# More seven-product rows, in alternation, with the weight sums made first

## The chip, the cores and the metric

The kernel runs on one core of a Trainium2 chip. The metric is the device time of one execution in microseconds; where several runs are shown, the median is meant. TensorE appears as PE (matmuls) and PEld (loads of the stationary operand), VectorE as DVE, ScalarE as ACT, GpSimd as POOL, SyncE as SP.

## The reference

One sequence of 256 positions and width 2048 goes through two layers: a retention layer, then a layer with multi-head latent attention, each followed by a squared-ReLU MLP of width 8192. All is float32.

```python
def sq_relu_mlp(h, w1, w2):
    return jnp.square(jax.nn.relu(h @ w1)) @ w2
...
    for layer in range(DEPTH):
        if layer < N_A_LAYERS:
            h = rms_norm(x, norm_mix[layer])
            x = x + retention(h, ret_w_in[layer], ret_w_out[layer], ret_cos, ret_sin)
        else:
            ...
            h = rms_norm(x, norm_mix[layer])
            x = x + mla_attention(h, mla_w_dq[j], mla_q_norm[j], mla_w_uq[j], mla_q_nope_norm[j],
                                  mla_q_pe_norm[j], mla_w_o[j], k_nope, k_pe, v, mla_cos, mla_sin)
        x = x + sq_relu_mlp(rms_norm(x, norm_mlp[layer]), mlp_w1[layer], mlp_w2[layer])
```

Retention has 8 heads (queries and keys of 256, values and gates of 512 a head) and an output product of 4096 x 2048. The weights are streamed from memory once; they make up nearly all of the traffic.

## The kernel before

Every product is made in split precision: each operand is taken apart into a rounded high part and a low part (the rest), and a product is three matmuls, high x high, high x low and low x high. Weights are split as they come in, in `split`: ScalarE rounds (the tile `wh`, line 183) and DVE subtracts (`wl`, line 184).

The big products go through `gemm_pair`: 256 positions by 1024 columns of output at a time, as 2 x 2 blocks (two tiles of 128 positions, two of 512 columns). The contracted dimension is passed in rows of 256, that is two k-tiles of 128 (in each row again 2 x 2 blocks of the weights); 2048 of it are 8 rows, numbered 0 to 7. Each row is one `quad`: one load of 1 MB into a `raw` tile, the splits, and the matmuls. An ordinary row makes 8 block products, 24 matmuls, each streaming 512 columns. A seven-product row uses Winograd's form of Strassen's scheme: 7 block products, 21 matmuls, out of sums of weight blocks (`u`, three DVE instructions, lines 312, 316 and 317) and sums of activation blocks (`with_sums`, lines 392 to 394, then a split; the tiles called `more`), which are made once for each activation tile that needs them. It takes four low splits (three of 1024 columns, one of 512) where an ordinary row takes two. Its partial results go to four further banks (`p1`, `p5`, and `p6` with `p7`), which `pair_out` combines with the others after the last row, in copies on ScalarE and sums on DVE.

Which rows are seven-product rows is given by tuples. `SEVEN` (rows 3, 5, 7) holds for most; the first `u` pair of an MLP, and the second half of the retention output, have 5 and 7 alone, since the sums of earlier rows aren't there in time. The attention products have tuples of their own, which the change leaves.

The stages in order, with the tile names that the profile shows: head 0 of the retention with plain products (`rg`, `rq`, `rk`, `rv`); for heads 1 to 7 query and key products (`rq`, `rk`) and a pair for gate and value (`rp`); after the projection of head 4 the first half of the output product (`ro`, two pairs), at the end the second half; the first MLP; key/value and query projections (`kd`, `dqp`, `dq`, `ku`, `uq`) with the attention; its output product (`wo`, `wop`); the second MLP. An MLP is done in four groups of 2048 hidden columns: two pairs of the up product (`u`, 8 rows each), then two pairs of the down product (`d`, 8 rows each). A down pair adds its result to x in device memory through GpSimd's queue (`to_home`); in the last group the first pair is added to x in SBUF (`into_x`), and the last 1024 columns are made by two plain products with three matmuls per k-tile and position tile (`gemm`, tile `d_acc`, weights `mlp_w2t`), one block of 512 columns after the other. When a block of x is complete, it is squared and summed for the norm, transposed, scaled and split for the next product (`x_block_t`).

Loads of weights are issued on SP's queue, in order. `raw` tiles have 3 buffers, `wh` and `wl` 5 each, `u` tiles 2, activation tiles (`act`) 24, general tiles of 2 KB (`f2k`) 14. Of the 8 banks, `tp` has 2, which transposes share with `p1` and `p5`; `p6`/`p7` share theirs with attention scores. Work that follows a product is put off by a queue that counts rows (`later(n, ...)` is n rows on, `tick` runs what is due, `need` runs it earlier where a product requires it). The framework's scheduler then orders the instructions of each engine, by program order and by what its model takes to be ready; it sets all waits. An engine runs its instructions in that order.

At the start the transposed x is loaded in 8 tiles (`first_inputs`) and split. Tiles 3, 5 and 7 are kept, scaled in place later, and their sums made (`sum_up`).

Of the kernel before, what the change touches and what calls it, by code (L numbers as in the profile page):

```python
# [43 lines left out]
NOPE, ROPE, MV, KVR, QR = 128, 64, 128, 512, 1536  # L44
KV_NBS, Q_NB = (320, 256), 384
GROUPS = (4, 4, 4, 4)
SEVEN = (3, 5, 7)
QUERY, FOUR = (3, 4, 6, 7), (3, 5, 6, 7)
PI = math.pi

# [16 lines left out]
def yoco(ctx: ExitStack, tc: tile.TileContext, a):  # L67
# [112 lines left out]
    def split(h, l, src, scale=None):  # L180

        if scale is None:
            nc.scalar.copy(h, src)  # L183
            nc.vector.tensor_tensor(l, src, h.bitcast(F32), op=ALU.subtract)  # L184
        else:
            nc.scalar.activation(h, src, AF.Copy, scale=scale)
            nc.vector.scalar_tensor_tensor(
                l, src, scale, h.bitcast(F32), op0=ALU.mult, op1=ALU.subtract
            )

    def split_act(v, src, scales=(None, None)):
        if scales == (None, None):
# [60 lines left out]
    def gemm_t(w, chunk0, act, nk, name, done):  # L253
# [3 lines left out]
        for g in range(n):  # L257
# [19 lines left out]

            stream(w, chunk0 + g, 2048, f"{name}{g}", use, (lambda: done(acc)) if g == n - 1 else None)

    def quad(w, chunk, x, mm, name):  # L280

        raw = pool.tile([P, 2048], F32, tag="raw", bufs=3, name=f"{name}_raw")
        nc.sync.dma_start(raw, w[chunk])
        v, more = x

        def a(t, k):
            return [v[:, k, i, t * P : (t + 1) * P] for i in range(2)]

        def s(n):
            return [more[:, n // 2, i, n % 2 * P : (n % 2 + 1) * P] for i in range(2)]  # L290

        def parts(src, n, part):
            wh = pool.tile([P, 1024], F32R, tag="wh", bufs=5, name=f"{name}_wh{part}")
            wl = pool.tile([P, 1024], F32R, tag="wl", bufs=5, name=f"{name}_wl{part}")
            split(wh[:, : n * 512], wl[:, : n * 512], src)
            return [[i[:, j * 512 : (j + 1) * 512] for i in (wh, wl)] for j in range(n)]

        if more is None:
            b11, b22 = parts(raw[:, 0:1024], 2, 0)
            mm("c11", a(0, 0), b11)  # L300
            mm("c21", a(1, 0), b11)
            mm("c12", a(0, 1), b22)
            mm("c22", a(1, 1), b22)
            b12, b21 = parts(raw[:, 1024:], 2, 1)
            mm("c12", a(0, 0), b12)
            mm("c22", a(1, 0), b12)
            mm("c11", a(0, 1), b21)
            mm("c21", a(1, 1), b21)
            return
        b11, b22 = parts(raw[:, 0:1024], 2, 0)  # L310
        u = [pool.tile([P, 2, 512], F32, tag="us", bufs=2, name=f"{name}_u{i}") for i in range(2)]
        nc.vector.tensor_tensor(
            u[0], raw[:, 0:1024].rearrange("p (i n) -> p i n", i=2),
            raw[:, 1024:1536].unsqueeze(1).to_broadcast([P, 2, 512]), op=ALU.add,
        )
        nc.vector.tensor_tensor(u[1][:, 0], u[0][:, 0], raw[:, 512:1024], op=ALU.add)
        nc.vector.tensor_tensor(u[1][:, 1], u[1][:, 0], raw[:, 1536:], op=ALU.add)  # L317
        mm("p1", a(0, 0), b11)
        mm("c12", s(3), b22)
        (b21,) = parts(raw[:, 1536:], 1, 1)  # L320
        mm("c11", a(0, 1), b21)
        u2, u4 = parts(u[1].rearrange("p i n -> p (i n)"), 2, 2)
        mm("c21", a(1, 1), u4)
        mm("p6", s(2), u2)
        u1, u3 = parts(u[0].rearrange("p i n -> p (i n)"), 2, 3)
        mm("p5", s(1), u1)
        mm("p7", s(0), u3)
# [243 lines left out]
    def first_inputs(c):  # L571

        t = f2k([2, S], f"x0t_{c}")
        nc.sync.dma_start(t, a["xt"][:, 2 * c : 2 * c + 2, :])
        v = act_tile(f"a0_{c}")
        split_act(v, t, [gain(G_MIX0 + 2 * c + j) for j in range(2)])
        act0.append(v)
        sums0.append(None)
        if c in SEVEN:

            def sum_up():
                for j in range(2):
                    nc.scalar.activation(t[:, j], t[:, j], AF.Copy, scale=gain(G_MIX0 + 2 * c + j))
                sums0[c] = with_sums(t, f"a0s_{c}")

            later(9 + c, sum_up)

# [68 lines left out]
    def ret_out(h, s, v, gate, y_act):  # L656
        o = two_banks(f"o{h}")
        ys = []
        for t in range(NT):
            for m in range(t + 1):  # L660
                lo = m * S + (t - m) * P
                sh, sl = (i[:, lo : lo + P] for i in s)
                vh, vl = v[m]
                nc.tensor.matmul(o[:, t], sh, vh, start=m == 0, stop=False)
                nc.tensor.matmul(o[:, t], sh, vl, start=False, stop=False)
                nc.tensor.matmul(o[:, t], sl, vh, start=False, stop=m == t)
        for t in range(NT):
            so = small(1, f"so{h}{t}")
            square_sum(o[:, t], so, f"o{h}{t}")
            ro = rstd(so, RDV, 1, f"o{h}{t}")  # L670
            y = f2k([512], f"y{h}{t}")
            nc.vector.scalar_tensor_tensor(y, o[:, t], ro, gate[t], op0=ALU.mult, op1=ALU.mult)
            ys.append(y)

        def turn():
            for k2 in range(2):
                tp = transposed(lambda t, j: ys[t][:, (2 * k2 + j) * P : (2 * k2 + j + 1) * P], f"ytp{h}{k2}")
                yt = act_tile(f"y{h}{k2}")
                more = None
                if len(y_act) in (SEVEN if h < RH // 2 else SEVEN[1:]):  # L680
# [12 lines left out]
    into_n1 = into_next(ss, [G_MLP0], [act], r, "n1", SEVEN)  # L693
    halves = [[], []]

    def ret_projected(h, qk, gate, v, s):
# [18 lines left out]
    def ret_out_half(i):  # L715

        w = a["ret_w_out"]
        if i:
            x_tiles("ro")
        for p in range(2):  # L720
            first = SEVEN[1:] if i else SEVEN

            def done(c, p=p):
                into_x(into_n1, c, p) if i else to_home(c, p)

            gemm_pair(w, p * 16 + 8 * i, halves[i], [k in first for k in range(8)], f"ro{i}{p}", done)

    for h in range(RH):
# [32 lines left out]
        if h == RH // 2:  # L761
            ret_out_half(0)
        need(r0, NT)
        while None in [sums0[k] for k in SEVEN]:
            run_first()
        gemm_pair(a["ret_w_gv"], (h - 1) * 8, list(zip(act0, sums0)), [k in SEVEN for k in range(8)], f"rp{h}", paired)
    ret_out_half(1)


    def mlp(layer, act, r, done):  # L770
        w1, w2 = a[f"mlp_w1_{layer}"], a[f"mlp_w2_{layer}"]
        f0 = 0
        for gi, nf in enumerate(GROUPS):
            hid, blocks = [], []
            kinds = [i in SEVEN for i in range(2 * nf)]
            last = gi == len(GROUPS) - 1

            def up(c, p, hid=hid, blocks=blocks):

                need(r, NT)  # L780
                c = summed(c)
                for t in range(NT):
                    for i in range(2):
                        nc.scalar.activation(c[t][i], c[t][i], AF.Relu, scale=r[t])

                def turn(i):
                    for q in (2 * i, 2 * i + 1):
# [8 lines left out]
                        blocks.append((v, with_sums(u, name) if len(blocks) in SEVEN else None))  # L796
                        hid.append(v)

                later(0, lambda: turn(0))
                later(1, lambda: turn(1))  # L800

            for p in range(f0 // 2, (f0 + nf) // 2):
                seven = SEVEN if p else SEVEN[1:]
                gemm_pair(
                    w1, p * 8, act, [i in seven for i in range(8)], f"u{layer}_{p}", lambda c, p=p, up=up: up(c, p)
                )
            if last:
                x_tiles(f"mlp{layer}")
            for p in range(2):
                if last and p:  # L810
                    for b in (2, 3):
                        need(hid, 2 * nf)
                        gemm(
# [5 lines left out]
                def add(c, p=p, last=last):  # L819
                    into_x(done, c, p) if last else to_home(c, p)  # L820

                gemm_pair(w2, p * 32 + 2 * f0, blocks, kinds, f"d{layer}_{gi}{p}", add)
            f0 += nf

# [245 lines left out]
    for b in range(8):  # L1070
# [3 lines left out]
    act, r = [], []  # L1074
    x_tiles("wo")
    gemm_blocks(
        a["mla_w_o"], lambda b: b * 4, a["mla_w_op"], o_act, KD, "wo", into_next(ss, [G_MLP1], [act], r, "n3", SEVEN)
    )

    def finish(b, acc):  # L1080
# [101 lines left out]
```

## Time and profile before

| | |
|---|---|
| runs | 2503.47, 2499.87, 2497.53 us; median 2499.87 |
| profiled execution | span 2497.0 us (the page gives no other time for it) |
| PE, PEld, DVE, ACT, POOL busy | 2471.9, 2075.1, 2096.7, 1574.8, 252.2 us |
| granted TensorE clock | 0.998 of full speed on average |
| memory | 478.09 MB read, 39.85 MB written |

The span is the time from the first to the last instruction of one execution. Busy times are the union of an engine's instructions. The recorded duration of a matmul (390 ns with 512 columns) is longer than the distance between two of them, since they are pipelined; the same holds, by less, for DVE's and ScalarE's instructions in a row. In a timeline "x3" stands for three instructions one after the other, and brackets show the idle time of the engine before an instruction and what ended it.

### The profile page before, as it was taken

The numbers are of one execution on the slowest core, as the hardware profiler recorded it, in microseconds if no ns is written. First come the engines' busy times: TensorE is split into PE (matmuls) and PEld (weight loads), VectorE is DVE, ScalarE is ACT, GpSimd is POOL, SyncE is SP. The second block draws the span as 40 slices with busy tenths as digits, with TensorE's granted clock in tenths as the row PEclk, the third lists the DMA queues.
The fourth block names the chain that finished last, engine by engine and source line by source line (L and its number), as shares of the span: only waits on it lengthen the run. The fifth ranks groups of instructions, "written<-read, shape, count | busy, mean of one in ns | idle before, by whom it ended". The sixth has DMA issues, their size and how long they took to land.

```text
span 2497.0 us, 31492 instructions
## 1 busy us (share of the span) xinstructions
PE 2471.9 (99%) x11683; PEld 2075.1 (83%) x11683; DVE 2096.7 (84%) x2723; ACT 1574.8 (63%) x2228; POOL 252.2 (10%) x308
## 2 busy tenths in 40 slices
PE   8999999999999999999999999999999999999999
PEld 7788888888888888888888888998888888888887
DVE  7788888888898888889889888776899888898896
ACT  6566555555676657566666767666676566575663
POOL 6300011000010110110110101110010201101100
PEclk9999999999999999999999999999999999999999
DMA  8545568555565685775875555444455956857754
GB/s 290 211 173 202 178 217 246 183 193 196 211 217 189 207 263 186 235 237 186 247 259 191 197 196 189 159 149 163 173 213 203 262 203 213 249 187 233 258 200 165
DMA packets 92825, 519.97 MB, mean 208 GB/s; under 512 B 11009, under 2 KB 12161, under 8 KB 39425
## 3 DMA queue, kind: packets, MB, share of 16 engines
q1 hardware_dynamic: 71280, 471.78, 52.5%
q0 software_dynamic: 21248, 46.15, 8.9%
q8 instruction: 91, 1.49, 0.2%
q14 instruction: 62, 0.50, 0.1%
q10 hardware_dynamic: 144, 0.05, 0.0%
HBM read 478.09 MB, written 39.85 MB: 207 GB/s over the span
## 4 chain that ended last, share of the span: by engine, by line
PE 80%; DVE 10%; DMA 4%; ACT 4%; issue 2%; POOL 1%; ACTq 0%; SPq 0%; DVEq 0%; POOLq 0%
PE u_c L353 7%; PE u_c L354 7%; PE u_c L352 7%; PE d_c L353 4%; PE d_c L354 4%; PE d_c L352 4%; PE rp_c L353 3%; PE rp_c L354 3%; PE rp_c L352 3%; DVE d_wl L184 3%; PE ro_c L352 2%; PE ro_c L353 2%; PE ro_c L354 2%; PE rq_acc L272 2%; PE rk_acc L272 2%; DMA d_raw<-in_mlp_w 2%
## 5 line engine op out<-in xcount | busy, mean ns | idle before, releaser
L184 DVE TENSOR_TENSOR u_wl<-u_raw,u_wh 128x1024 fp32r<-128x1024 f32 (+1 forms) x256 | 280.0, 1124 | 35.8 <-ACT u_wh L183 35.8
L184 DVE TENSOR_TENSOR d_wl<-d_raw,d_wh 128x1024 fp32r<-128x1024 f32 (+1 forms) x256 | 283.4, 1132 | 26.0 <-ACT d_wh L183 25.1
L353 PE MATMUL u_c<-u_wl,n 128*128 128x512 f32 x748 | 291.8, 390 | 1.1 <-DVE u_wl L184 1.0
L352 PE MATMUL u_c<-u_wh,n 128*128 128x512 f32 x748 | 291.3, 391 | 0.0
L354 PE MATMUL u_c<-u_wh,n 128*128 128x512 f32 x748 | 291.3, 389 | 0.0
L183 ACT CAST u_wh<-u_raw 128x1024 fp32r<-128x1024 f32 (+1 forms) x256 | 238.9, 981 | 60.6 <-DMA u_raw<-in_mlp_w 27.2
L183 ACT CAST d_wh<-d_raw 128x1024 fp32r<-128x1024 f32 (+1 forms) x256 | 240.0, 991 | 56.3 <-DMA d_raw<-in_mlp_w 25.1
L353 PE MATMUL d_c<-d_wl,hid 128*128 128x512 f32 x644 | 251.4, 390 | 1.7 <-DVE d_wl L184 1.6
L352 PE MATMUL d_c<-d_wh,hid 128*128 128x512 f32 x644 | 252.1, 391 | 0.0
L354 PE MATMUL d_c<-d_wh,hid 128*128 128x512 f32 x644 | 250.9, 390 | 0.0
L183 ACT CAST u_wh<-u_u 128x1024 fp32r<-128x1024 f32 x92 | 94.2, 1050 | 153.5 <-DVE u_u L317 129.8
L183 ACT CAST d_wh<-d_u 128x1024 fp32r<-128x1024 f32 x84 | 84.9, 1049 | 162.6 <-DVE d_u L317 154.7
L353 PEld LDWEIGHTS u_c<-u_wl,n 128*128 128x128 f32 x748 | 140.5, 188 | 31.1 <-DVE u_wl L184 2.8
L354 PEld LDWEIGHTS u_c<-u_wh,n 128*128 128x128 f32 x748 | 140.4, 188 | 29.2
L352 PEld LDWEIGHTS u_c<-u_wh,n 128*128 128x128 f32 x748 | 140.4, 188 | 28.6
L183 ACT CAST rp_wh<-rp_raw 128x1024 fp32r<-128x1024 f32 x112 | 106.7, 972 | 67.7 <-PE rp_c L354 37.5
L184 DVE TENSOR_TENSOR u_wl<-u_u,u_wh 128x1024 fp32r<-128x1024 f32 x92 | 110.7, 1222 | 43.6 <-ACT u_wh L183 43.5
L353 PEld LDWEIGHTS d_c<-d_wl,hid 128*128 128x128 f32 x644 | 120.9, 188 | 29.0 <-DVE d_wl L184 4.5
L354 PEld LDWEIGHTS d_c<-d_wh,hid 128*128 128x128 f32 x644 | 120.9, 188 | 25.1
L352 PEld LDWEIGHTS d_c<-d_wh,hid 128*128 128x128 f32 x644 | 120.9, 188 | 24.6
L184 DVE TENSOR_TENSOR d_wl<-d_u,d_wh 128x1024 fp32r<-128x1024 f32 x84 | 99.9, 1222 | 35.9 <-ACT d_wh L183 35.9
L148 POOL DMA_DIRECT2D xh<-d_c x48 | 42.1, 1029 | 844.6 <-ACT d_c L369 844.5
(567 smaller groups left out, 6570.0 us busy)
## 6 DMA issues: line engine op xcount, KB each, us to landing
u_raw<-in_mlp_w SPq DMA_DIRECT2D x128, 1024.0 KB, 5.3
d_raw<-in_mlp_w SPq DMA_DIRECT2D x112, 1024.0 KB, 4.9
rp_raw<-in_ret_w_gv SPq DMA_DIRECT2D x56, 1024.0 KB, 4.9
ro_raw<-in_ret_w_out SPq DMA_DIRECT2D x32, 1024.0 KB, 4.9
uq_raw<-in_mla_w_uq SPq DMA_DIRECT2D x24, 768.0 KB, 4.1
rq_raw<-in_ret_w_qk SPq DMA_DIRECT2D x16, 1024.0 KB, 6.6
rk_raw<-in_ret_w_qk SPq DMA_DIRECT2D x16, 1024.0 KB, 4.8
d_raw<-in_mlp_w2t SPq DMA_DIRECT2D x16, 1024.0 KB, 5.1
```

The lines of the kernel that those rows point to most:

```text
L148: nc.gpsimd.dma_start(x_home[t][2 * p + j], part, accum_op=ALU.add)
L183: nc.scalar.copy(h, src)
L184: nc.vector.tensor_tensor(l, src, h.bitcast(F32), op=ALU.subtract)
L272: nc.tensor.matmul(acc[f], wh[:, cols], a.rearrange("p i s -> p (i s)"), start=k == 0, stop=k == nk - 1)
L352: nc.tensor.matmul(dst, ah, bh, start=n == 0, stop=False)
L353: nc.tensor.matmul(dst, ah, bl, start=False, stop=False)
L354: nc.tensor.matmul(dst, al, bh, start=False, stop=n == total[key] - 1)
```

## The change

1. Further tuples: `LATE` (5, 7), `ODD` (1, 3, 5, 7), `HEAD` (2, 4, 6, 7). `LATE` is what `SEVEN[1:]` was.
2. Retention: the gate and value pairs and the first half of the output product take `HEAD` instead of `SEVEN`. The sums of x at the start are made for tiles 2, 4, 6 and 7, and the tile is loaded a second time for it rather than kept.
3. MLP, up: pairs 1, 3, 5 and 7 keep `SEVEN`, pairs 2, 4 and 6 take `ODD`, pair 0 has `LATE` as before. MLP, down: the first pair of a group keeps `SEVEN`, the second takes `ODD`. Activation sums are made for `ODD`, that is one more in each group and one more for the input of each MLP.
4. The end of the first MLP: its last 1024 columns are made by a pair with `LATE` instead of two plain products, and go to x as those of the first pair do. The second MLP ends as before.
5. In a seven-product row the three sums of weights are written first, and the first two low splits get an edge that orders them behind the last sum on DVE. It is an order alone and no semaphore.

```diff
-SEVEN = (3, 5, 7)
+SEVEN, LATE, ODD, HEAD = (3, 5, 7), (5, 7), (1, 3, 5, 7), (2, 4, 6, 7)
...
+    def queued_behind(ins, before):
+        tc.add_manual_dep(
+            ins.ins, before.ins.name,
+            mybir.DependencyInfo(mybir.DependencyClass.NoSync, mybir.DependencyReason.DATA), reason="order",
+        )
...
-        def parts(src, n, part):
+        def parts(src, n, part, after=None):
             wh = pool.tile([P, 1024], F32R, tag="wh", bufs=5, name=f"{name}_wh{part}")
             wl = pool.tile([P, 1024], F32R, tag="wl", bufs=5, name=f"{name}_wl{part}")
-            split(wh[:, : n * 512], wl[:, : n * 512], src)
+            low = split(wh[:, : n * 512], wl[:, : n * 512], src)
+            if after is not None:
+                queued_behind(low, after)
...
-        b11, b22 = parts(raw[:, 0:1024], 2, 0)
         u = [pool.tile([P, 2, 512], F32, tag="us", bufs=2, name=f"{name}_u{i}") for i in range(2)]
...
-        nc.vector.tensor_tensor(u[1][:, 1], u[1][:, 0], raw[:, 1536:], op=ALU.add)
+        summed_up = nc.vector.tensor_tensor(u[1][:, 1], u[1][:, 0], raw[:, 1536:], op=ALU.add)
+        b11, b22 = parts(raw[:, 0:1024], 2, 0, summed_up)
         mm("p1", a(0, 0), b11)
         mm("c12", s(3), b22)
-        (b21,) = parts(raw[:, 1536:], 1, 1)
+        (b21,) = parts(raw[:, 1536:], 1, 1, summed_up)
...
-        if c in SEVEN:
+        if c in HEAD:
 
             def sum_up():
+                again = f2k([2, S], f"x0s_{c}")
+                nc.sync.dma_start(again, a["xt"][:, 2 * c : 2 * c + 2, :])
...
-                seven = SEVEN if p else SEVEN[1:]
+                seven = SEVEN if p % 2 else ODD if p else LATE
...
-                if last and p:
+                if last and p and layer:
...
+                kinds = [i in ((LATE if last else ODD) if p else SEVEN) for i in range(2 * nf)]
                 gemm_pair(w2, p * 32 + 2 * f0, blocks, kinds, f"d{layer}_{gi}{p}", add)
```

More of the change, by code (lines that the diff above doesn't have):

```diff
@@ L183, in split @@
             nc.scalar.copy(h, src)
[L184 to L189, printed above, removed]
+            return nc.vector.tensor_tensor(l, src, h.bitcast(F32), op=ALU.subtract)
+        nc.scalar.activation(h, src, AF.Copy, scale=scale)
+        return nc.vector.scalar_tensor_tensor(
+            l, src, scale, h.bitcast(F32), op0=ALU.mult, op1=ALU.subtract
+        )
     def split_act(v, src, scales=(None, None)):
@@ L278, in gemm_t @@
             stream(w, chunk0 + g, 2048, f"{name}{g}", use, (lambda: done(acc)) if g == n - 1 else None)
+    def queued_behind(ins, before):
+        tc.add_manual_dep(
+            ins.ins, before.ins.name,
+            mybir.DependencyInfo(mybir.DependencyClass.NoSync, mybir.DependencyReason.DATA), reason="order",
+        )
     def quad(w, chunk, x, mm, name):
@@ L578, in first_inputs @@
         sums0.append(None)
-        if c in SEVEN:
+        if c in HEAD:
             def sum_up():
+                again = f2k([2, S], f"x0s_{c}")
+                nc.sync.dma_start(again, a["xt"][:, 2 * c : 2 * c + 2, :])
                 for j in range(2):
-                    nc.scalar.activation(t[:, j], t[:, j], AF.Copy, scale=gain(G_MIX0 + 2 * c + j))
-                sums0[c] = with_sums(t, f"a0s_{c}")
+                    nc.scalar.activation(again[:, j], again[:, j], AF.Copy, scale=gain(G_MIX0 + 2 * c + j))
+                sums0[c] = with_sums(again, f"a0s_{c}")
             later(9 + c, sum_up)
@@ L679, in turn @@
                 more = None
-                if len(y_act) in (SEVEN if h < RH // 2 else SEVEN[1:]):
+                if len(y_act) in (HEAD if h < RH // 2 else LATE):
                     u = f2k([2, S], f"yu{h}{k2}")
@@ L692, in yoco @@
     act, r = [], []
-    into_n1 = into_next(ss, [G_MLP0], [act], r, "n1", SEVEN)
+    into_n1 = into_next(ss, [G_MLP0], [act], r, "n1", ODD)
     halves = [[], []]
@@ L720, in ret_out_half @@
         for p in range(2):
-            first = SEVEN[1:] if i else SEVEN
+            first = LATE if i else HEAD
             def done(c, p=p):
@@ L763, in yoco @@
         need(r0, NT)
-        while None in [sums0[k] for k in SEVEN]:
+        while None in [sums0[k] for k in HEAD]:
             run_first()
-        gemm_pair(a["ret_w_gv"], (h - 1) * 8, list(zip(act0, sums0)), [k in SEVEN for k in range(8)], f"rp{h}", paired)
+        gemm_pair(a["ret_w_gv"], (h - 1) * 8, list(zip(act0, sums0)), [k in HEAD for k in range(8)], f"rp{h}", paired)
     ret_out_half(1)
@@ L774, in mlp @@
             hid, blocks = [], []
-            kinds = [i in SEVEN for i in range(2 * nf)]
             last = gi == len(GROUPS) - 1
@@ L795, in turn @@
                         split_act(v, u)
-                        blocks.append((v, with_sums(u, name) if len(blocks) in SEVEN else None))
+                        blocks.append((v, with_sums(u, name) if len(blocks) in ODD else None))
                         hid.append(v)
@@ L1076, in yoco @@
     gemm_blocks(
-        a["mla_w_o"], lambda b: b * 4, a["mla_w_op"], o_act, KD, "wo", into_next(ss, [G_MLP1], [act], r, "n3", SEVEN)
+        a["mla_w_o"], lambda b: b * 4, a["mla_w_op"], o_act, KD, "wo", into_next(ss, [G_MLP1], [act], r, "n3", ODD)
     )
@@ L1168 @@
         arrays[f"mlp_w2_{i}"] = _quads(g["mlp_w2"][i])
-        arrays[f"mlp_w2t_{i}"] = _chunks(g["mlp_w2"][i][-512 * GROUPS[-1] :, 1024:], 512)
+    arrays["mlp_w2t_1"] = _chunks(g["mlp_w2"][1][-512 * GROUPS[-1] :, 1024:], 512)
     arrays = {n: np.ascontiguousarray(v) for n, v in arrays.items()}
```

## Prediction

> **What bounds the kernel now.** I read the page first, then busy time by stage, then one stretch of eleven microseconds instruction by instruction, and last the waits. From the page:
>
> ```profile
> span 2497.0 us, 31492 instructions
> PE 2471.9 (99%) x11683; PEld 2075.1 (83%) x11683; DVE 2096.7 (84%) x2723; ACT 1574.8 (63%) x2228; POOL 252.2 (10%) x308
> ...
> PE 80%; DVE 10%; DMA 4%; ACT 4%; issue 2%; POOL 1%; ACTq 0%; SPq 0%; DVEq 0%; POOLq 0%
> ```
>
> PE is busy throughout, and the chain that ended last is PE for 80% and DVE for 10%. So fewer matmuls are worth their time, as long as DVE, the second engine, still delivers. Busy time by stage, for one head's gate and value pair, the first half of the retention output, two `u` pairs, two `d` pairs (columns: window, length, then busy time and instructions of each engine):
>
> ```profile
> core 0: us, PE busy (x) PEld busy (x) DVE busy (x) ACT busy (x) POOL busy (x), PEclk, DMA share, GB/s
> 464.00:507.00 43.00, 43.00 (x196) 35.72 (x195) 34.09 (x41) 23.53 (x30) 0.00 (x0) 1.00 0.49 181
> 312.00:397.00 85.00, 85.00 (x383) 70.59 (x382) 69.65 (x80) 49.13 (x61) 9.52 (x12) 1.00 0.70 221
> 906.00:991.00 85.00, 85.00 (x385) 70.56 (x384) 73.81 (x82) 54.02 (x70) 4.73 (x6) 1.00 0.66 219
> 991.00:1076.00 85.00, 84.97 (x382) 69.92 (x381) 74.90 (x87) 54.34 (x71) 9.14 (x11) 1.00 0.72 227
> ```
>
> PE fills every stage at full clock; DVE has 10 to 11 us of 85 left in the MLP. Whether those are free is seen in the timeline of DVE, over one ordinary and one seven-product row of a `d` pair:
>
> ```profile
> 1012.64 3.49 DVE L184 TENSOR_TENSOR d_wl<-d_raw,d_wh 128x1024 fp32r<-128x1024 f32 x3
> 1016.04 1.22 DVE L312 TENSOR_TENSOR d_u<-d_raw 128x1024 f32<-128x1024 f32 x1
> 1017.18 0.68 DVE L184 TENSOR_TENSOR d_wl<-d_raw,d_wh 128x512 fp32r<-128x512 f32 x1
> 1017.78 0.68 DVE L316 TENSOR_TENSOR d_u<-d_u,d_raw 128x512 f32<-128x512 f32 x1
> 1018.50 0.69 DVE L317 TENSOR_TENSOR d_u<-d_u,d_raw 128x512 f32<-128x512 f32 x1
> 1020.38 2.36 DVE L184 TENSOR_TENSOR d_wl<-d_u,d_wh 128x1024 fp32r<-128x1024 f32 x2 [1.19 <-ACT d_wh L183]
> 1022.66 3.49 DVE L184 TENSOR_TENSOR d_wl<-d_raw,d_wh 128x1024 fp32r<-128x1024 f32 x3
> ```
>
> The three low splits at the start are two of the ordinary row and the first of the seven-product row: 3.40 us to the next start, 1.13 each. The last sum (L317) ends at 1019.19; then DVE idles 1.19 us, because ScalarE can only now round the sums, and ScalarE had itself waited for them:
>
> ```profile
> 1019.30 2.00 ACT L183 CAST d_wh<-d_u 128x1024 fp32r<-128x1024 f32 x2 [4.74 <-DVE d_u L317]
> ```
>
> Period of DVE for the two rows: 1022.66 - 1012.64 = 10.02 us, 8.83 of it work. The same two rows on PE:
>
> ```profile
> 1014.25 0.39 PE L352 MATMUL d_c<-d_wh,hid 128*128 128x512 f32 x1
> ...
> 1019.69 0.39 PE L352 MATMUL d_p<-d_wh,hid 128*128 128x512 f32 x1
> 1019.91 0.39 PE L353 MATMUL d_p<-d_wl,hid 128*128 128x512 f32 x1
> ...
> 1021.95 0.39 PE L353 MATMUL d_c<-d_wl,hid 128*128 128x512 f32 x1
> ...
> 1024.45 0.39 PE L352 MATMUL d_c<-d_wh,hid 128*128 128x512 f32 x1
> ```
>
> The ordinary row starts at 1014.25, the seven-product row at 1019.69, the next row at 1024.45: 5.44 us for 24 matmuls, 4.76 us for 21, 0.2267 us a matmul, 10.20 together. So in alternating rows DVE's 10.02 us barely keep up with 10.20: the low part of the sums is finished at about 1021.6 (the first of the two splits that begin at 1020.38), and PE uses it at 1021.95. The 10% of DVE in the chain are such stretches. More seven-product rows alone would not fit; the order of the sums has to make room.
>
> **The matmuls removed.** Seven-product rows, before and after: gate and value pairs 7 x 3 to 7 x 4 (+7); first half of the retention output 2 x 3 to 2 x 4 (+2); `u`, per layer, 2 + 7 x 3 = 23 to 2 + 4 x 3 + 3 x 4 = 26 (+3, both layers +6); `d` of the first layer 7 x 3 = 21 to 4 x 3 + 3 x 4 + 2 = 26 (+5); `d` of the second 21 to 24 (+3). That is 23 rows, three matmuls fewer in each: 69 x 0.2267 = 15.6 us off PE. Two of the 23 are in the pair at the end of the first MLP, whose other 6 rows have as many matmuls as the two plain products they replace (2 x 96 against 186).
>
> **What DVE gets for it.** From the timeline a seven-product row costs DVE 1.13 + 1.14 + 0.60 + 0.72 + 0.69 + 2.28 = 6.56 us, an ordinary one 2.27: 4.29 more for each added row. A further set of activation sums costs, by the rows of its four steps,
>
> ```profile
> L392 DVE TENSOR_TENSOR hid_sum<-hid_u 128x256 f32<-128x256 f32 x24 | 10.0, 418 | 0.0
> L393 DVE TENSOR_TENSOR hid_sum<-hid_sum,hid_u 128x128 f32<-128x128 f32 x24 | 6.8, 284 | 0.0
> L394 DVE TENSOR_TENSOR hid_sum<-hid_u,hid_sum 128x128 f32<-128x128 f32 x24 | 6.8, 284 | 0.0
> L184 DVE TENSOR_TENSOR hid_more<-hid_sum,hid_more 128x512 fp32r<-128x512 f32 x24 | 16.4, 685 | 0.0
> ```
>
> 0.42 + 0.28 + 0.28 + 0.69 = 1.67 us; there are 12 more of them (one in each of the eight MLP groups, one each for x0, y and the inputs of the two MLPs). Take a group of the MLP, two `u` and two `d` pairs: PE 170.0 - 2 x 0.68 = 168.6 us; DVE 73.8 + 74.9 + 2 x 4.29 + 1.67 = 159.0. It fits with 9.6 us to spare, which is 0.69 us for each of the 14 seven-product rows in it. A gate and value stage: DVE 34.1 + 4.3 = 38.4 of 42.3. ScalarE has 54 of 85 busy and gets some 1.5 us more a row (two casts of 1.00 more, 0.5 less): no bound.
>
> **The order of the sums.** The new edges put the sums ahead of the row's first two low splits. ScalarE then rounds the raw blocks while DVE adds, and rounds the sums while DVE makes the two low splits (1.13 + 0.60 = 1.73 us against 1.00 for the first cast). The idle 1.19 us has work in it, and two alternating rows cost DVE 8.83 us instead of 10.02, against 10.20 on PE. This is the cover for everything above. In the page's terms, these waits go:
>
> ```profile
> DVE u_wl L184 <- ACT u_wh L183: 79.4, 82, 2.4
> DVE d_wl L184 <- ACT d_wh L183: 60.9, 68, 2.5
> ```
>
> What is queued behind the sums on DVE: the row's low splits, then the next row's, then the sums of `pair_out`. Waiting for that are PE's second matmul in the row, and SP's next load, as its slot of `raw` is free only when two low splits and three sums have read it; that is 1.13 + 1.14 + 0.60 + 0.72 + 0.69 = 4.3 us into the row, before and after. PE's second matmul gets its operand later by the three sums (1.14 + 0.60 + 0.69 = 2.43 us): it was ready at 1016.13 (third split of the group), it is used at 1019.91. 3.8 us of lead become 1.4. Nothing is lost here, but this is where a smaller lead would show.
>
> DVE is tightest where a pair with 1,3,5,7 follows another: rows 7, 0, 1 with the four sums of `pair_out` between (128x512 like L316, some 0.6 each) cost 2 x 6.56 + 2.27 + 2.4 = 17.8 us against 4.76 + 5.44 + 4.76 = 15.0. The 2.8 us come out of the lead, which the alternating rows before it raise by 10.20 - 8.83 = 1.4 us per two rows. Stalls on PE there: between -3 us (those of today go) and +5 over the kernel; I take -1, as the cadence is the nearest row.
>
> **The end of the first MLP.** Now blocks 2 and 3 end together. The nearest rows are the end of the retention output, a pair, and of today's plain product (PE's last matmul, then the last add to x, then the first scaled tile of block 3 for the key/value product):
>
> ```profile
> 733.28 0.39 PE L354 MATMUL ro_p<-ro_wh,y_more 128*128 128x512 f32 x1
> ...
> 742.97 0.68 DVE L461 TENSOR_TENSOR x_ro<-ro_p,x_ro 128x512 f32<-128x512 f32 x1
> ...
> 1423.43 0.39 PE L246 MATMUL d_acc<-d_wh,hid 128*128 128x512 f32 x1
> 1423.65 0.30 PE L244 MATMUL kd_acc<-kd_wh,n 128*128 128x320 f32 x1
> ...
> 1424.32 0.68 DVE L461 TENSOR_TENSOR x_mlp<-d_acc,x_mlp 128x512 f32<-128x512 f32 x1
> ...
> 1427.17 1.04 PE L203 MATMUL n_tp<-cst,x_mlp 128*128 128x128 f32 x8
> ...
> 1429.89 0.48 DVE L187 SCALAR_TENSOR_TENSOR n<-n_tp,gains,n 128x256 fp32r<-128x256 f32 x1 [0.54 <-ACT n L186]
> ```
>
> A pair's x is complete 10.0 us after its last matmul (743.65 - 733.67), a plain product's 1.2 (1425.00 - 1423.82), and a scaled tile follows 5.4 us later (1430.37). So block 3 is late by 8.8 us. As cover, PE has the key/value product of blocks 0 and 1: 24 matmuls took 3.52 us (1423.65 to 1427.17), so 48 take 7.0, and as much again less a fifth in the second, narrower one. Nothing if both are drawn ahead; up to 8 us if PE keeps the order written. I take 3, nearer to the end at which the scheduler moves work, as it did with the low splits above.
>
> **The start.** Four tiles of x are loaded again (256 KB each) on SP, ahead of weights, where three were kept. SP's wait for the sums there goes:
>
> ```profile
> SPq L283 <- DVE a0s_sum L393: 10.1, 1, 10.1
> ```
>
> but the new loads can wait for a free f2k slot. From -1 to +3; I take 0.
>
> Sum: 2497.0 - 15.6 - 1 + 3 = 2483.4 for the span. The median of the runs, 2499.9, is 2.9 above the span; the page has no other time for the profiled run. Forecast 2486.3; by the low ends (-3, 0, -1) 2480, by the high ones (+5, +8, +3) 2500.
>
> **The rivals.** (1) The waits stay. If the reordered row still costs DVE more than 0.69 us of waiting (today 1.19), DVE becomes the bound of the MLP, and each tenth above that costs 8 groups x 14 rows x 0.1 = 11 us. At 1.0 us that is 35 over the forecast: 2521. For it: the edge gives only an order, and a scheduler that lays other work between keeps the ping-pong. Against it: all that the casts need is ready 1.7 us earlier. At 0.8 us, 12 us are lost and no gain can be measured: 2499.
>
> (2) The first low part is late. DVE runs its queue in order, so a row entered with under 2.4 us of lead pays the rest. 84 seven-product rows lie in pairs or stages that get a fourth one (48 in the MLPs, 28 and 8 in the retention); at 0.3 us each that is 25 us, 2511. It decides from 0.19 us a row on. Against it: leads like the 3.8 us above.
>
> (3) DVE's instructions cost their recorded 1.22 us and not the 1.13 between starts, that is 159.0 x 1.08 = 171.7 us in a group of 168.6 on PE: 8 x 3.1 = 25 us lost, 2511. The Trainium skill, "VectorE: DVE Perf Modes", section on the DRAIN that can't be avoided, has the next instruction start only when the pipe is empty (unless it is not held, a case that its next section adds); its fp32 two-tensor formula, (N+151)/0.96, gives 1224 ns for 1024 elements. The recorded 1.22 agrees with the formula, the spacing of 1.13 does not agree with the rule, and the spacing is measured.
>
> (4) The tail and the start take their high ends (8 and 3): 2494.
>
> **How the numbers follow.** About 0.2%, 5 us, is what a measurement of this kernel can tell from no change. Forecast with its bounds 0.70 (all of it faster); rival 1 0.13 (half of it within 0.2%, half slower); rival 2 0.08 (0.06 slower, 0.02 within); rival 3 0.03 slower; rival 4 0.06 (0.03 faster, 0.03 within). Faster 0.73, same 0.11, slower 0.16 by rounding. The range goes from 2479, just under the low ends, to 2505; what lies outside is most of the slower cases and 0.03 below.
>
> **What would show it.** PE 69 instructions of 128x512 fewer in the pairs; in the timeline of DVE the three sums ahead of the row's low splits and no wait for ScalarE before the splits of the sums; the waits of `u_wl` and `d_wl` for `u_wh` and `d_wh` much below 140 us together; DVE near 2200 us busy; a `u` pair stage some 0.7 us shorter for each added row. Wrong: gaps on PE before the second matmul of a seven-product row (rival 2), DVE idle behind ScalarE still (rival 1), a gap of over 5 us in the key/value product.

## Result and profile after

| | before | after |
|---|---|---|
| median of the runs, us | 2499.93 (2497.34 to 2503.47) | 2501.86 (2492.71 to 2505.62) |
| ratio | | 1.0006, 95% interval 0.9996 to 1.0017 |
| profiled execution, us | span 2497.0 | 2504.95, span 2503.2 |
| granted clock | 0.998 | 0.997 |

No change that can be measured; the forecast was 2486.3. From the page of the changed kernel, its totals and the shares of the chain that ended last:

```profile
span 2503.2 us, 31661 instructions
PE 2458.7 (98%) x11614; PEld 2065.5 (83%) x11614; DVE 2199.6 (88%) x2892; ACT 1647.8 (66%) x2297; POOL 252.0 (10%) x308
PE 76%; DVE 12%; DMA 7%; issue 2%; ACT 2%; POOL 1%; DVEq 0%; SPq 0%; ACTq 0%; POOLq 0%
```

PE has the 69 instructions less (11683 to 11614), yet the span of this execution is 6.2 us longer (it is one of the slower of twelve; the medians differ by 1.9). In the chain PE's share fell from 80% to 76%, and DMA's rose from 4% to 7%. Cut at PE's first matmul into `u_c`, its first into `kd_acc`, its next into `u_c` and the end of its last, the two executions compare so (us; "forecast" is the number of added seven-product rows by 0.68, and the +3 of the pair at the end; the -1 for stalls had no place):

| part | before | after | change | forecast |
|---|---|---|---|---|
| retention | 733.5 | 728.2 | -5.3 | -6.1 |
| first MLP | 690.1 | 694.8 | +4.7 | -5.4 |
| key/value, query, attention | 381.0 | 381.9 | +0.9 | +3 |
| second MLP | 688.2 | 693.7 | +5.5 | -4.1 |

So the loss lies in the MLPs, 19.7 us against the forecast for the two. By stages (16 rows, two `u` or two `d` pairs, from PE's first matmul of one to that of the next), a `u` stage that now holds a pair with 1,3,5,7 took 84.76 us before where PE had no gap (in the first MLP 84.76, 84.76 and 86.27). With one row more and no gap it would take 84.08. In the first MLP the three of them took 86.20, 88.39 and 89.17. Busy time in stretches of the first two and of the `d` stage behind them; the columns are those of the prediction's table:

```profile
901.00:987.00 86.00, 84.18 (x380) 69.55 (x379) 77.30 (x89) 57.48 (x73) 4.68 (x6) 1.00 0.67 216
1073.00:1161.00 88.00, 85.78 (x379) 70.46 (x379) 78.36 (x91) 57.27 (x72) 4.43 (x6) 0.98 0.65 212
1161.00:1245.00 84.00, 84.00 (x380) 69.69 (x379) 78.48 (x93) 57.68 (x73) 9.07 (x11) 1.00 0.75 228
```

In the `d` stage PE is busy without a gap; it took 84.09 us. In the two `u` stages PE is idle for 1.8 and 2.2 us, and DVE, which is what PE waits for, has 9 to 10 us idle in each. What ended the idle time (columns: who waited, at which line, and for what; us in total, times, longest):

```profile
DVE d_wl L184 <- ACT d_wh L183: 30.7, 31, 3.0
DVE u_u L318 <- DMA u_raw<-in_mlp_w: 30.0, 17, 4.4
DVE u_wl L184 <- ACT u_wh L183: 26.5, 29, 1.5
DVE d_u L318 <- DMA d_raw<-in_mlp_w: 25.6, 16, 3.5
PE u_c L360 <- DVE u_wl L184: 11.7, 6, 3.1
PE d_c L360 <- DVE d_wl L184: 7.8, 5, 2.4
```

and the four rows of before that answer to the last ones:

```profile
DVE u_u L312 <- DMA u_raw<-in_mlp_w: 6.9, 9, 3.0
DVE d_u L312 <- DMA d_raw<-in_mlp_w: 2.3, 4, 0.8
PE d_c L353 <- DVE d_wl L184: 1.6, 4, 0.5
PE u_c L353 <- DVE u_wl L184: 1.0, 2, 0.8
```

The waits for ScalarE's casts went as predicted, 140.3 us to 57.2. In their place the first sum of a seven-product row (L318) waits for its load: 9.2 us became 55.6. And PE waits for low parts: 2.6 us became 19.5. One such place in the timeline of DVE, then ScalarE, PE, and the pieces of the chain there:

```profile
1087.94 2.35 DVE L184 TENSOR_TENSOR u_wl<-u_u,u_wh 128x1024 fp32r<-128x1024 f32 x2
1093.12 1.23 DVE L318 TENSOR_TENSOR u_u<-u_raw 128x1024 f32<-128x1024 f32 x1 [2.82 <-DMA u_raw<-in_mlp_w]
1094.38 0.69 DVE L322 TENSOR_TENSOR u_u<-u_u,u_raw 128x512 f32<-128x512 f32 x1
1094.99 2.35 DVE L184 TENSOR_TENSOR u_wl<-u_raw,u_wh 128x1024 fp32r<-128x1024 f32 x2
1097.26 0.68 DVE L323 TENSOR_TENSOR u_u<-u_u,u_raw 128x512 f32<-128x512 f32 x1
1097.86 1.82 DVE L184 TENSOR_TENSOR u_wl<-u_raw,u_wh 128x1024 fp32r<-128x1024 f32 x2
```

```profile
1089.13 1.06 ACT L183 CAST u_wh<-u_raw 128x1024 fp32r<-128x1024 f32 x1 [0.73 <-PE u_c L361]
1090.45 1.05 ACT L183 CAST u_wh<-u_raw 128x1024 fp32r<-128x1024 f32 x1 [0.26 <-PE u_c L361]
```

```profile
1093.65 0.39 PE L359 MATMUL u_c<-u_wh,n 128*128 128x512 f32 x1
1096.26 0.51 PE L360 MATMUL u_c<-u_wl,n 128*128 128x512 f32 x1 [2.23 <-DVE u_wl L184]
```

```profile
1084.99 8.04 DMA u_raw<-in_mlp_w
...
1093.12 1.24 DVE u_u L318
```

PE waits 2.23 us for the first of the two splits at 1094.99. They belong to the ordinary row before the seven-product row. ScalarE had cast that row by 1090.19 and 1091.50, so its low splits could have run from 1090.3 on, when DVE became idle. But the scheduler had put the first two sums of the next row ahead of them, and DVE takes its queue in order: it waited until 1093.1 for a load of 1 MB that took 8.04 us, with ready work behind the wait. The last sum (L323) came behind those splits after all, so the row's sums are not even together. All eleven pauses of PE for low parts in the MLPs have this pattern: a load of 7.3 to 9.6 us, then the first two sums (L318, L322), then the ready splits, and PE goes on 3.2 us after the load has landed. In before, the splits of the ordinary row stand ahead of the sums (the prediction's timeline, 1012.64).

### The profile page after: what moved, and what is told of

Its sections match the earlier page's. It is cut to its first block, busy times and chain, and to the rows that moved or that the text cites. A ratio compares the mean times of both kernels' runs of the same rounds, so it can differ in the third digit from the quotient of the medians.

```text
span 2503.2 us, 31661 instructions
## 1 busy us (share of the span) xinstructions
PE 2458.7 (98%) x11614; PEld 2065.5 (83%) x11614; DVE 2199.6 (88%) x2892; ACT 1647.8 (66%) x2297; POOL 252.0 (10%) x308
## 4 chain that ended last, share of the span: by engine, by line
PE 76%; DVE 12%; DMA 7%; issue 2%; ACT 2%; POOL 1%; DVEq 0%; SPq 0%; ACTq 0%; POOLq 0%
PE u_c L360 6%; PE u_c L361 6%; PE u_c L359 6%; PE d_c L360 4%; PE d_c L361 4%; PE d_c L359 4%; DMA d_raw<-in_mlp_w 3%; DVE d_wl L184 3%; DMA u_raw<-in_mlp_w 3%; PE rp_c L360 2%; PE rp_c L359 2%; PE rp_c L361 2%; PE rq_acc L271 2%; PE rk_acc L271 2%; DVE u_wl L184 2%
## 5 line engine op out<-in xcount | busy, mean ns | idle before, releaser
L360 PE MATMUL u_c<-u_wl,n 128*128 128x512 f32 x712 | 280.0, 393 | 11.7 <-DVE u_wl L184 11.7
L359 PE MATMUL u_c<-u_wh,n 128*128 128x512 f32 x712 | 280.4, 395 | 0.0
L361 PE MATMUL u_c<-u_wh,n 128*128 128x512 f32 x712 | 279.1, 392 | 0.0
L360 PE MATMUL d_c<-d_wl,hid 128*128 128x512 f32 x660 | 258.1, 391 | 7.8 <-DVE d_wl L184 7.8
L359 PE MATMUL d_c<-d_wh,hid 128*128 128x512 f32 x660 | 259.1, 393 | 0.0
L361 PE MATMUL d_c<-d_wh,hid 128*128 128x512 f32 x660 | 257.6, 390 | 0.0
L183 ACT CAST u_wh<-u_u 128x1024 fp32r<-128x1024 f32 x104 | 107.8, 1054 | 115.2 <-PE u_c L361 59.2
L183 ACT CAST d_wh<-d_u 128x1024 fp32r<-128x1024 f32 x100 | 103.6, 1055 | 101.0 <-DVE d_u L323 57.5
L361 PEld LDWEIGHTS u_c<-u_wh,n 128*128 128x128 f32 x712 | 134.9, 189 | 28.2
L359 PEld LDWEIGHTS u_c<-u_wh,n 128*128 128x128 f32 x712 | 134.8, 189 | 27.4
L361 PEld LDWEIGHTS d_c<-d_wh,hid 128*128 128x128 f32 x660 | 124.3, 188 | 25.8
L359 PEld LDWEIGHTS d_c<-d_wh,hid 128*128 128x128 f32 x660 | 124.3, 188 | 25.3
L184 DVE TENSOR_TENSOR u_wl<-u_u,u_wh 128x1024 fp32r<-128x1024 f32 x104 | 124.2, 1220 | 9.8 <-ACT u_wh L183 9.8
L184 DVE TENSOR_TENSOR rp_wl<-rp_raw,rp_wh 128x1024 fp32r<-128x1024 f32 x112 | 118.9, 1090 | 3.8 <-ACT rp_wh L183 3.2
```

What stands on the lines that cost most here:

```text
L184: return nc.vector.tensor_tensor(l, src, h.bitcast(F32), op=ALU.subtract)
L359: nc.tensor.matmul(dst, ah, bh, start=n == 0, stop=False)
L360: nc.tensor.matmul(dst, ah, bl, start=False, stop=False)
L361: nc.tensor.matmul(dst, al, bh, start=False, stop=n == total[key] - 1)
```

## Theories

**A**: the loss is this place of the sums, ahead of ready splits of the row before, together with loads that land late. **B**: DVE has too much work with the added rows. **C**: three load buffers are too few, since slots come free later. The expectations below use these letters.

## Experiments

Intervals are 95%, and each ratio is to the kernel before on the same chip.

**1. The sums behind the row before.** One more edge of the same kind: the first sum of a row is ordered behind the last low split of the row before.

```diff
+    row_before, low_split = [None], [None]
...
+        row_before[0] = low_split[0]
...
+            low_split[0] = low
...
-        nc.vector.tensor_tensor(
+        first_sum = nc.vector.tensor_tensor(
...
+        if row_before[0] is not None:
+            queued_behind(first_sum, row_before[0])
```

> The changed kernel with one more order edge: the first sum of a seven-product row stands behind the last low split of the row before it. Theory A (the sums were moved ahead of low splits of the row before, whose operands are ready, and DVE then waits for the load of the seven-product row with these splits behind it): DVE's idle time ended by loads of u_raw and d_raw falls from some 55 us to under 20, PE's waits in the MLPs by 15 to 20 us, time 2485 to 2490. Theory B (DVE has too much work, 2200 us busy): no change, 2497 to 2505. Theory C (three load buffers are too few for the faster rows, whatever DVE's order): the waits for loads move from the sums to the splits, 2495 to 2502.

Measured: 2478.61 (2476.24 to 2479.91), ratio 0.9917 (0.9902 to 0.9931). Its page, the row that is left of the sums' waits for loads in the MLPs, the same `u` stage, and DVE at the same place:

```profile
span 2476.1 us, 31659 instructions
PE 2449.7 (99%) x11614; PEld 2061.9 (83%) x11614; DVE 2207.3 (89%) x2892; ACT 1646.1 (66%) x2297; POOL 253.8 (10%) x308
```

```profile
DVE u_u L322 <- DMA u_raw<-in_mlp_w: 1.6, 3, 0.7
```

```profile
1069.00:1153.00 84.00, 84.00 (x381) 69.73 (x380) 78.98 (x92) 57.49 (x73) 4.90 (x6) 1.00 0.71 222
```

```profile
1086.65 2.39 DVE L184 TENSOR_TENSOR u_wl<-u_raw,u_wh 128x1024 fp32r<-128x1024 f32 x2
1089.33 1.23 DVE L322 TENSOR_TENSOR u_u<-u_raw 128x1024 f32<-128x1024 f32 x1 [0.30 <-DMA u_raw<-in_mlp_w]
1090.60 0.69 DVE L328 TENSOR_TENSOR u_u<-u_u,u_raw 128x512 f32<-128x512 f32 x1
1091.32 0.69 DVE L329 TENSOR_TENSOR u_u<-u_u,u_raw 128x512 f32<-128x512 f32 x1
1091.93 1.82 DVE L184 TENSOR_TENSOR u_wl<-u_raw,u_wh 128x1024 fp32r<-128x1024 f32 x2
```

Here the two splits of the ordinary row stand first, then the three sums, then the row's own splits. The sums wait 1.6 us for loads instead of 55.6, its list has no wait of `u_c` or `d_c` for a low part, and the `u` stage that took 88.39 us takes 84.08, as does every `u` and `d` stage of the first MLP but its first and last. The first MLP is 679.2 us instead of 694.8, the second 678.8 instead of 693.7. B falls: DVE has slightly more work here (2207.3 us) and PE runs without gaps. C falls: the buffers are the same. The gain, 23 us of median, is larger than A expected.

**2. The tuples without the change's edges.**

```diff
-            if after is not None:
-                queued_behind(low, after)
```

> The changed kernel without the order edges (the sums are still written first). Theory A: the wait of DVE for ScalarE's rounding of the sums comes back where the scheduler puts the low splits first, and the sums ahead of the row before stay in part: 2500 to 2515. Theory B: no difference to the changed kernel, 2497 to 2505, as the work of DVE is the same. Theory C: the same as B.

Measured: 2485.90 (2483.52 to 2490.52), ratio 0.9947 (0.9932 to 0.9962): faster than expected, a miss. Without the edges the sums stay behind the row before, and DVE waits for the casts instead:

```profile
DVE d_wl L184 <- ACT d_wh L183: 52.5, 51, 1.5
DVE u_wl L184 <- ACT u_wh L183: 48.4, 49, 1.8
```

These waits total 100.9 us over 100 times, none above 1.8 us, and PE's lead covers nearly all of them: but for the first and the last of each MLP, the stages take 84.08 to 84.56 us. So the rest of the change, the added rows with the sums written first, is worth 14 us without the edges, and the edges took 16 us away. How the 14 divide between the rows and the place of the sums in the program isn't shown here. The room that I thought the edges had to make was there without them.

**3. The order alone, with the old rows.** The kernel before with the three sums first and the change's edges (`queued_behind` and `summed_up` as in the diff above), old tuples and old end.

> The kernel before with the sums first and the edges, and nothing else of the change (rows, end of the first MLP and loads at the start as before). Theory A: the sums wait for loads with ready splits behind them here too, but DVE has 100 us less to do and more lead: 2495 to 2503, with DVE's idle time ended by loads of u_raw and d_raw at 20 to 40 us instead of 13. Theory B: DVE is relieved of its waits for ScalarE, PE's waits in the MLPs fall: 2488 to 2494. Theory C: as before, 2497 to 2502.

Measured: 2485.91 (2483.40 to 2487.53), ratio 0.9945 (0.9931 to 0.9959): B's number was nearer than A's. The misplaced sums wait here too, but PE hardly does:

```profile
DVE u_u L318 <- DMA u_raw<-in_mlp_w: 28.2, 20, 3.0
DVE d_u L318 <- DMA d_raw<-in_mlp_w: 21.9, 14, 3.0
PE u_c L360 <- DVE u_wl L184: 1.3, 2, 0.7
PE d_c L360 <- DVE d_wl L184: 1.3, 2, 0.9
```

Against 50.1 us of waiting on DVE, PE waits 2.6 us for low parts, and the two MLPs take 1373.1 us against 1368.3 with the sums in the right place (experiment 7). So A needs an addition: the misplaced sums cost much only where DVE's lead is short. That the lead is longer here because DVE has 2096 us of work in place of 2200 is an inference from these totals.

**4. The retention part alone.** The rows, the order and the start of the retention as changed; the MLPs, their end and the first query pair (its name begins with `d`, too) as before.

```diff
-            if after is not None:
+            if after is not None and name[0] not in "ud":
...
-                seven = SEVEN if p % 2 else ODD if p else LATE
+                seven = SEVEN if p else LATE
```

> Rows 2, 4, 6, 7 and the sums first in the retention alone; the MLPs and the first query pair have rows, order, sums of activations and end of the kernel before. Nine seven-product rows more, 6.1 us of PE. All theories: 2492 to 2496, as the loss lies in the MLPs; if it is 2498 or more the loss lies in the retention.

Measured: 2496.61 (2491.16 to 2503.76), ratio 0.9987 (0.9976 to 0.9999), 3.6 us under before and just above the expectation. By the medians the retention is not where the loss is. The trace doesn't show the gain: the profiled execution was the slowest of twelve (2503.76), and its retention took 733.9 us.

**5. The end of the first MLP as before**, on top of experiment 1 (two plain products; the last group's second `d` pair goes).

```diff
-                if last and p and layer:
+                if last and p:
...
-                kinds = [i in ((LATE if last else ODD) if p else SEVEN) for i in range(2 * nf)]
+                kinds = [i in (ODD if p else SEVEN) for i in range(2 * nf)]
```

> As e1, but the first MLP ends with two plain products as before. By the trace of e1 the pair leaves 3.6 us of waits in the key/value product where the kernel before has 0.1, and saves 6 matmuls (1.4 us) and about 1 us of waits in the plain products: 1 to 2 us faster than e1, 2476 to 2478. If the pair's end is hidden, 1 to 2 us slower than e1, 2480 to 2481.

Measured: 2474.07 (2472.64 to 2474.56), ratio 0.9897 (0.9878 to 0.9916), span 2472.6: the fastest version that computes everything. By parts, first MLP and attention together take 1060.8 us against 1062.6 in experiment 1. So the pair costs 1.8 us net there, after the 1.4 us that its two seven-product rows save; 3.2 gross. A closer cut gives more: the two products behind the pair (`kd`, `dqp`) took 74.6 us in experiment 1 and 69.0 here, and the first MLP is 2.2 us shorter in experiment 1, so 3.4 net and 4.8 gross. The rest of the 4.5 us between the medians isn't put down to the pair. Experiment 1 shows one place of the pair's price:

```profile
PE kd_acc L244 <- DVE kd_wl L184: 2.2, 2, 1.3
```

**6. The new edge alone**, without the change's two: experiment 1 with the edit of experiment 2.

> As e1, without the two edges of the change: only the first sum is held behind the row before, the low splits of the row itself come where the scheduler puts them. If the change's own edges are worth their cause (no wait for ScalarE's rounding of the sums): 5 to 10 us slower than e1, 2484 to 2489, with DVE's waits for u_wh and d_wh some 40 us above those of e1. If all that matters is that no ready split waits behind a sum: within 2 us of e1.

Measured: 2520.0 (2516.59 to 2524.29), ratio 1.0082 (1.0063 to 1.01): slower, a clear miss, and 34 us above experiment 2, which lacks this edge as well. These waits of this kernel tell of a part of it:

```profile
ACT u_wh L183 <- DVE u_u L327: 141.2, 36, 5.5
ACT d_wh L183 <- DVE d_u L327: 135.6, 35, 5.5
...
ACT u_c L380 <- PE u_c L365: 34.3, 10, 4.4
ACT d_c L380 <- PE d_c L365: 34.1, 9, 4.4
```

In experiment 1 the first two are 145.5 us together in place of 276.8, and the last two 15.9 in place of 68.4, never above 0.6 us. ScalarE now stands in its queue before a copy of a bank that PE has not finished, with casts behind it: a fault of the same kind on another engine. The MLPs are 8 and 9 us longer than in experiment 1; another 18 us went in the retention and 8 in the attention, whose order changed too. I have not separated these. Each edge changes all that the scheduler chooses after it, so an edge has no price of its own.

**7. Both orders with the old rows**: experiment 3 with the edge of experiment 1.

> The kernel before with both orders of e1 (sums behind the row before, the row's first low splits behind the sums), rows and ends as before. Against e1 this tells what the 23 rows are worth when the order is right: 69 matmuls are 15.6 us, less some 2 us at the end of the first MLP and some 3 at the start, so 2488 to 2490 by the matmuls. It has PE's waits of the start and attention left, as e3 had: by e3 (2485.9) it is 2482 to 2486, and the rows are then worth only 4 to 8.

Measured: 2484.31 (2482.79 to 2486.85), ratio 0.9939 (0.9924 to 0.9955), as expected from experiment 3 and below the count by matmuls. Against experiment 5, which has the same end, the added rows are worth 10.2 us; 21 of them remain there, 14.3 us of matmuls. By parts the two MLPs give all of theirs (1360.2 us against 1368.3, 8.1 of 8.2), and what is missing lies in the retention (1.9 of 6.1; the attention, which has no added row, differs by another 2.9 us between these two executions). Without them the better place of the sums brings little (2485.91 to 2484.31), which fits the addition to A.

**8. The changed kernel without the transfers that add to x in memory.** The body of `to_home` is empty, so the sums of these pairs are left out of x: 112 transfers of 256 KB on GpSimd's queue are gone.

> The changed kernel without the additions to x in device memory (to_home does nothing, so 96 transfers of 256 KB that read and write are gone and the sums of these pairs are left out of x). Theory A (DVE waits for late loads with ready splits behind): loads land earlier, PE's waits in the MLPs fall from 27 to under 12 us, 2483 to 2490. If the order of DVE's work alone costs the time, whether loads are late or not: 2497 to 2503.

Measured: 2473.39 (2472.98 to 2474.68), ratio 0.9896 (0.9877 to 0.9915), more than A expected. Its waits of the sums for loads, and DVE where the sums stand ahead of the splits:

```profile
DVE u_u L315 <- DMA u_raw<-in_mlp_w: 3.8, 4, 1.4
DVE d_u L315 <- DMA d_raw<-in_mlp_w: 1.3, 1, 1.3
```

```profile
1081.61 1.22 DVE L315 TENSOR_TENSOR u_u<-u_raw 128x1024 f32<-128x1024 f32 x1
1082.86 0.69 DVE L319 TENSOR_TENSOR u_u<-u_u,u_raw 128x512 f32<-128x512 f32 x1
1083.47 2.35 DVE L181 TENSOR_TENSOR u_wl<-u_raw,u_wh 128x1024 fp32r<-128x1024 f32 x2
```

DVE's 2892 instructions come in the same order as in the changed kernel, the two sums ahead of the splits and the third behind, and so do ScalarE's 2297 and PE's 11614. Now the load is there, and next to nothing waits: 5.1 us instead of 55.6, and all `u` stages but the first of each MLP take 84.08 us. So the misplaced sums and the late loads are both needed for the loss. The loads are late in the other versions as well: of the 256 loads of MLP weights (1 MB each), those in flight together with an accumulating transfer took 7.5 us in the median in the changed kernel (74 of them; the others 4.9), 7.6 in before and 7.5 in experiment 1. Of loads above 7 us there are 53, 53 and 62, and 10 without the transfers. Each of the eleven pauses follows such an overlapped load.

**9 and 10. The same cut in the kernel before, and in experiment 1** (again the sums of these pairs are left out of x). They ask if the transfers simply cost every version some 28 us.

> The kernel before, without the transfers that add to x in memory (the sums of these pairs are left out of x). Theory A (the loss of the changed kernel is ready splits queued behind sums that wait for a load, and the accumulating transfers make the loads late): the kernel before loses its time to the ping-pong of DVE and ScalarE, which has nothing to do with loads, so it gains little: only its waits of u_u and d_u for loads (9 us of DVE, 1 to 2.6 us of PE) and some of the spread; 2490 to 2498. The rival, that the accumulating transfers cost every version the same 25 to 28 us, by the memory traffic or by the banks and buffers that they hold: 2470 to 2477.

> The changed kernel with the sums ordered behind the row before, and without the transfers that add to x in memory (the sums of these pairs are left out of x). Theory A: with the loads early, the place of the sums no longer matters, and with the place mended the loads no longer matter; so it comes out within 3 us of the changed kernel without the transfers (2473.4) and at most 6 us under the one with the order alone (2478.6): 2472 to 2477. The rival, that the two repairs are separate gains that add up (23 and 28 us): 2450 to 2460, which is far below what PE's own work allows, or at least under 2468.

Measured: 2492.13 (2489.2 to 2493.63), ratio 0.9971 (0.9961 to 0.9982), and 2476.87 (2475.68 to 2477.84), ratio 0.9914 (0.99 to 0.9927). The first is as A expected; the second is in the range that A gave, though 3.5 us above experiment 8 where A had said 3 at most. Without the transfers before gains 7 us, experiment 1 under 2, and the changed kernel 28. The two repairs don't add: the MLPs take 679.3 and 678.9 us in experiment 8, 679.2 and 678.8 in experiments 1 and 10. They remove the same loss. How the transfers make loads late (shared DMA engines, the memory, or the banks and tiles that they hold) is not separated.

## Why the prediction was wrong

Point by point:

- **Matmuls removed**: right. 69 fewer; one added row makes a `u` stage 0.68 us shorter where nothing waits, 84.08 us in experiment 1 against 84.76.
- **What DVE gets**: right. 2199.6 us busy against "near 2200", and experiment 1 shows that it fits.
- **Waits for the casts**: right, 140.3 us to 57.2. But that alone brought nothing: experiment 2 keeps 100.9 us of them and is 16 us faster.
- **The end of the first MLP**: +3 taken, 3.2 to 4.8 measured with experiments 1 and 5.
- **The start**: 0 taken, and too low. The retention gained 5.3 us of the 6.1 forecast, but 2.0 of that lie ahead of its second product, a stretch that takes 29.7 to 32.6 us over the versions whatever their rows. From there to the end of the first gate and value pair it took 118.6 us before and 119.3 after, with a row less: a price of 1.4 us. Between experiments 7 and 5 it is 117.4 to 121.4, a price of 4.7, above the bound of +3; it is what the rows of experiment 7 miss.
- **Stalls**: the step that failed. "Stalls on PE there: between -3 us (those of today go) and +5 over the kernel; I take -1, as the cadence is the nearest row." It was about +20 (the MLPs' 19.7 us above), because low splits that were ready stood on DVE behind sums that waited for late loads. The waits of `u_c` and `d_c` for low parts rose by 16.9, and the lower clock behind four of them added 6.8 (last section); that is 4 us more than 19.7, which fits stalls of before that went. The low end was short too: with the old rows the two MLPs take 1368.3 us in experiment 7 against 1378.3 before, so the stalls that could go were 10 us and not 3. This fits experiments 1 and 5, which come out below the forecast.

The error lies in one sentence: "What is queued behind the sums on DVE: the row's low splits, then the next row's". I looked only behind the sums, inside the order that was written. Nothing in the edges says how early the sums may go, and the splits of the row before ended up behind them. I also took the load as landed: the 9.2 us of waits for loads in before stand in its list of waits, and they were the place to look.

Rival 2 came nearest: an in-order DVE queue, and gaps on PE before the second matmul of a row. But it had a steady 0.3 us in every row; the trace shows eleven waits of up to 3.1 us, and the low part that came late is the ordinary row's. Rival 1 fell, since the waits for ScalarE went down to 57.2 us and none of the eleven pauses comes from one. Rival 3 fell: at its price DVE would need 171.7 us a group, and in experiment 1 two stages, a group, take 168.2. Of rival 4, the end's price stayed near the value taken, and the start's passed its high end between experiments 7 and 5. Summed by parts, the forecast differs from the trace by 19.7 us in the MLPs, by 0.8 in the retention and by -2.1 in the attention.

## What to carry to other kernels

An edge that puts B behind A says nothing about how early A may go: before adding one, list what stands ahead of A in its engine's queue, and bind A from that side too if it depends on a load. Work that waits for a transfer belongs behind work that is ready, on every engine that runs in order. When a reordering is costed, read the waits for loads as well as the wait that it removes, because a queue's lead is shared by both.

## What was not expected of the hardware

A stall of PE can cost more than its length. In the trace of the changed kernel, four of the pauses in the MLPs are followed by matmuls at about half speed. Windows behind three pauses, one of them short (the clock is the third number from the end):

```profile
1096.00:1100.00 4.00, 3.74 (x10) 2.95 (x11) 4.00 (x6) 1.05 (x1) 0.00 (x0) 0.58 0.38 104
1269.40:1274.40 5.00, 4.91 (x14) 3.87 (x15) 4.65 (x6) 1.79 (x2) 0.00 (x0) 0.66 0.49 179
923.80:927.80 4.00, 3.89 (x17) 3.23 (x18) 4.00 (x6) 2.06 (x2) 0.00 (x0) 1.00 0.42 121
```

```profile
1096.99 0.63 PE L359 MATMUL u_c<-u_wh,n 128*128 128x512 f32 x1
...
1099.55 0.62 PE L359 MATMUL u_c<-u_wh,n 128*128 128x512 f32 x1
```

From 1096.99 to 1099.55 there are six steps from one matmul to the next, 0.427 us each in place of 0.227. A clock of 0.58 over 4 us loses 4 x 0.42 = 1.7 us, and 0.66 over 5 us the same: four times 1.7, that is 6.8 us. They followed pauses of 2.4 to 3.2 us (the distance between two starts, less the usual 0.227); pauses of 0.8 to 2.0 us in the MLPs had none. In experiment 6 one came behind a pause of 1.8 us with shorter ones, 0.2 to 0.5 us, on both sides of it, so the length of one pause may not be all that counts. The Trainium skill, "TensorE: Matmul & The Clock Gate", Part 1, has a gate that goes to half rate after an idle window of about 3.4 us; its half-rate spacing of 426.7 ns agrees with the 0.427 us here, while here 2.4 us of pause were enough.

The other is that DVE's order alone does not set the time: the same order of 2892 instructions ran in 2501.86 us and, without the accumulating transfers, in 2473.39.
